# w_down's block sums by accumulating transfers from GpSimd, and another order of the seven products

## The chip, the cores and the metric

The kernel runs on one core of one Trainium2 chip. The metric is the device time of one execution in microseconds; the time before is the median of three runs. A core has five engines that run side by side and wait for each other by semaphores: PE (TensorE, matrix products into PSUM banks), DVE (VectorE), ACT (ScalarE), POOL (GpSimd) and SP (SyncE, which here issues nearly all transfers). PEld is the loading of the stationary operand for PE.

## The reference, cut to what matters

Two layers of a hybrid decoder on a sequence of 512 rows, width 1024, all in float32. Each layer has three parallel branches (a state-space scan, latent attention, a gated delta rule), a gated merge, and then the feed forward, which is what the change touches:

```python
D_MODEL = 1024; SEQ = 512; DEPTH = 2; D_FF = 4 * D_MODEL

    h = x + mixed @ w_out
    f = jnp.square(jax.nn.relu(rmsnorm(h, norm2_g) @ w_up)) @ w_down
    return h + f
```

`w_up` is 1024 x 4096 and `w_down` 4096 x 1024 in each layer.

## The kernel before

Every float32 operand of a product is split into a high part and a rest (`split_half`, lines 170 and 171: ACT casts `whi`, DVE subtracts to get `wlo`), and each product of two blocks is three matmuls (`mm3`, lines 200, 203, 204). The buffers of `whi` and `wlo` are four each, so ACT and DVE run up to four splits ahead of PE, and the cast of a split waits until PE has done with the split four places before it.

The feed forward runs in four quarters of the hidden width, `qd` = 0 to 3, per layer. A quarter is `up(qd)`, four chunks of w_up, and then `seven(...)`: the 512 x 1024 activations times a 1024 x 1024 part of w_down, done with seven products of 512 x 512 blocks instead of eight, with sums of blocks on either side. In w_down's part, the blocks (i, j) are held in tiles `wr00` (called b11), `wr01`, `wr10` (b21), `wr11` (b22), each 128 x 4 x 512, 1 MB. The sums on this side are

- p1 = (0,0) + (0,1), in tile `wp1`, made by DVE in `after(2)` of `seven_weights` (line 1200)
- p3 = (0,1) + (1,1), in place in `wr01`, made by DVE in `after(3)` (line 1200)
- p2 = p1 + (1,1), in two tiles `f` (`halves`, line 1262)
- p4 = p2 + (1,0), written back into `wp1` (`plus4`, line 1275)

Each is two DVE operations of 128 x 1024. `after(c)` is called behind each of up's four chunks and also issues the load of a block on SP (line 1208).

The products are named by their activation operand. Before, their order was a11, a12, s2, s1, s3, s4, a22, and in quarter 3 (`early`) a11, a12, s1, s2, s4, s3, a22. Two pairs of PSUM banks take them: a11, s2, s3 and a22 accumulate in the pair `x`, s1 and s4 in the pair `z`, and a12 has a pair of small banks of its own. After each product DVE adds both of its banks to h or subtracts them (line 1244). A product that goes on in the same pair may start on a bank only when that operation has read it. Within a product the first bank's matmuls and the second's take turns, three each, over four blocks k; so a product is 24 matmuls.

w_out's product of each layer uses `seven` in the same way (with `mid`), and keeps its form.

The program's order on each engine is set by a scheduler that goes by priorities; tiles with one buffer (`wp1`, `wr..`) are given to the next quarter when the last reader is done.

Of the kernel before, what the change touches and what calls it, by code (L numbers as in the profile page):

```python
# [10 lines left out]
F32 = mybir.dt.float32  # L11
# [4 lines left out]
ALU = mybir.AluOpType  # L16
# [4 lines left out]
P = 128  # L21
S = 512
T = S // P
D = 1024
# [31 lines left out]
def hybrid_kernel(ctx, tc, a, out, depth=2, taps=None):  # L56
    nc = tc.nc
    pe, act, dve, pool, sync = nc.tensor, nc.scalar, nc.vector, nc.gpsimd, nc.sync
    uid = itertools.count()

    def mk(pl, shape, dt, tag, bufs=None):
        return pl.tile(shape, dt, tag=tag, name=f"{tag}_{next(uid)}", bufs=bufs)
# [24 lines left out]
    def acc_bank():  # L87
        return mk(ps_acc, [P, 512], F32, "acc")
# [4 lines left out]
    def sm_bank():  # L93
        return mk(ps_sm, [P, 512], F32, "sm")
# [55 lines left out]
    def after_product(i, o):  # L150
        tc.add_manual_dep(i, o.name, order_only, reason="behind a product")

    def behind(key, ins):

        if key in seen_at:
            after_product(ins.ins, seen_at[key])
        else:
            awaiting.setdefault(key, []).append(ins.ins)

    def place(key, ins):  # L160
        seen_at[key] = ins.ins
        for i in awaiting.pop(key, ()):
            after_product(i, ins.ins)

    def split_half(raw, hold=None, first=True, at=None):

        n = raw.shape[1]
        hi, lo = hold or (mk(wp, [P, n], F32R, "whi"), mk(wp, [P, n], F32R, "wlo"))
        with tc.high_priority() if first else nullcontext():
            act.copy(hi, raw)  # L170
            x = dve.tensor_tensor(lo, raw, f32(hi), ALU.subtract)  # L171
            if at:
                behind(at, x)
        return hi, lo
# [116 lines left out]
    def square(o, x, pl, tag, bufs=2, scale=1.0):  # L291
        jk = mk(pl, [P, 512], F32, tag, bufs)[:, : x.shape[-1]]
        act.activation(jk, x, AF.Square, scale=scale, accum_out=o)
# [97 lines left out]
    for ly in range(depth):  # L391
# [206 lines left out]
        for hp in range(4):  # L598
# [61 lines left out]
            for k, wh, wl in wkv:  # L660
                for t in range(T):
                    tok = slice(t * P, (t + 1) * P)
                    o = pss[t // 2][:, t % 2 * 256 : t % 2 * 256 + 256]
                    ah, al, bh, bl = ckh[k][:, tok], ckl[k][:, tok], vcols(wh[:, 0, :]), vcols(wl[:, 0, :])
                    more = t % 2 == 1
                    x = pe.matmul(o, ah, bh, start=k == 0 and not more, stop=False, skip_group_check=more)
# [9 lines left out]
            for j in range(2):  # L676
# [3 lines left out]
                for t in range(T):  # L680
                    n = max(256, (t + 1) * P)
                    tok = slice(t * P, (t + 1) * P)
                    ps = sm_bank()
                    o = ps[:, :n]
# [5 lines left out]
                    n = (t + 1) * P  # L690
                    o = ps[:, :n]
# [9 lines left out]
                for kbs in ((0,), (1,), (3, 2)):  # L701
                    ps = sm_bank()
                    n = 0
# [14 lines left out]
                    for kb, c0, c in parts:  # L718
                        v_h, v_l = (x[:, kb % 2, j, :] for x in vs[kb // 2])
                        o = po[:, c0:]  # L720
# [451 lines left out]
        rows = itertools.count()  # L1172
# [18 lines left out]
        hpl = h_pool.enter_context(tc.tile_pool(name="hp", bufs=1, reuse_waits="tile"))  # L1191
        last = ly == depth - 1
        ssq = [mk(sp, [P, 2], F32, "nss", 4) for _ in range(T)]
        def seven_weights(pl, w2d, r0, sums_at=None):

            b = {}

            def plus(o, x, y):
                for q in (slice(0, 1024), slice(1024, 2048)):
                    z = dve.tensor_tensor(o[:, q], x[:, q], y[:, q], ALU.add)  # L1200
                    if sums_at:
                        behind(sums_at, z)

            def after(c):
                i, j = ((0, 0), (0, 1), (1, 1), (1, 0))[c]
                b[i, j] = mk(pl, [P, 4 * 512], F32, f"wr{i}{j}")
                rows, cols = (slice(o + 512 * e, o + 512 * (e + 1)) for o, e in ((r0, i), (0, j)))
                sync.dma_start(b[i, j].rearrange("p (k n) -> p k n", k=4), w2d[rows, cols].rearrange("(k p) n -> p k n", p=P))
                if c == 2:
                    b["p1"] = mk(pl, [P, 4 * 512], F32, "wp1")  # L1210
                    plus(b["p1"], b[0, 0], b[0, 1])
                if c == 3:
                    plus(b[0, 1], b[0, 1], b[1, 1])

            return b, after

        def seven(pl, ops, b, sq=None, before_last=None, fin=None, nf=4, pre=None, mid=None, prep=None, early=False, tag=None, settled=None, rest=None):

            x, z = ([acc_bank() for _ in range(2)] for _ in range(2))

            def product(ps, n, raw, start, i, j, op, done):

                w = []
                if pre:
                    pre(n)
                rowwise = sq and (done == 2 or (rest and n == "s3"))
                for k in range(4):
                    if pre and n == "s2" and k == 2:
                        pre("s4")
                    w.append(split_half(raw(k)))  # L1230
                    if rowwise:
                        continue
                    for t in range(2):
                        mul(ps, n, w, k, t, start)
                for t in range(2):
                    if rowwise:
                        for k in range(4):
                            mul(ps, n, w, k, t, start)
                    r = 2 * i + t
                    if r == 3 and rest and done == 2:  # L1240
                        return rest(ps[t])
                    hs_ = h[:, r, j * 512 : (j + 1) * 512]
                    with tc.high_priority():
                        place((tag, n, t), dve.tensor_tensor(hs_, hs_, ps[t], op))  # L1244
                    if done and sq:
                        square(sq[r][:, j : j + 1], hs_, pl, "fs", 3 if nf == 4 else 2, D ** -0.5 if settled else 1.0)
                        if settled and i == j:
                            settled(r, j)
                        if done == 2 and fin:
                            fin(r)  # L1250

            def mul(ps, n, w, k, t, start):
                ah, al = (o[:, k % 2 * 256 + t * P : k % 2 * 256 + (t + 1) * P] for o in ops[n][k // 2])
                key = (tag, "s4", 3, 1) if tag and early and n == "s3" and k == 0 else None
                place((tag, n, k, t), mm3(ps[t], ah, al, *w[k], start and k == 0, k == 3, not start, key))

            b11, p3, b21, b22, p1 = (b[n] for n in ((0, 0), (0, 1), (1, 0), (1, 1), "p1"))

            halves = [mk(pl, [P, 2 * S], F32, "f", nf) for _ in range(2)]
            for q, o in enumerate(halves):  # L1260
                cs = slice(q * 1024, (q + 1) * 1024)
                dve.tensor_tensor(o, p1[:, cs], b22[:, cs], ALU.add)
            if prep:
                prep()
            p2 = lambda k: halves[k // 2][:, k % 2 * 512 : k % 2 * 512 + 512]
            of = lambda o: lambda k: o[:, k * 512 : (k + 1) * 512]
            product(x, "a11", of(b11), True, 0, 0, ALU.add, 0)
            if mid:
                mid()
            product([sm_bank() for _ in range(2)], "a12", of(b21), True, 0, 0, ALU.add, 1)  # L1270
            p4 = mk(pl, [P, 4 * 512], F32, "wr00") if mid else p1

            def plus4(q):
                cs = slice(q * 1024, (q + 1) * 1024)
                dve.tensor_tensor(p4[:, cs], halves[q], b21[:, cs], ALU.add)

            later = [lambda: plus4(0), lambda: plus4(1)]
            for n in ("s1", "s2", "s4", "s3") if early else ("s2", "s1", "s3", "s4"):
                if n == "s1":
                    product(z, n, of(p1), True, 1, 1, ALU.add, 0)  # L1280
                if n == "s2":
                    product(x, n, p2, False, 0, 1, ALU.subtract, 0)
                if n == "s3":
                    product(x, n, of(p3), False, 1, 1, ALU.subtract, 1)
                if n == "s4":
                    product(z, n, of(b22), False, 0, 1, ALU.add, 1)
                if later and n in ("s2" if early else "s1", "s4" if early else "s3"):
                    later.pop(0)()
            if before_last:
                before_last()  # L1290
            product(x, "a22", of(p4), False, 1, 0, ALU.add, 2)

        with tc.tile_pool(name="wo", bufs=1, reuse_waits="tile") as wo:
# [12 lines left out]
            b, after = seven_weights(wo, a["w_out"][ly], 0)  # L1306
# [135 lines left out]
        with tc.tile_pool(name="ff", bufs=1, reuse_waits="tile") as fp:  # L1442
# [50 lines left out]

            def down_weights(qd):

                return seven_weights(fp, a["w_down"][ly], qd * D, None if qd else ((ly, "u", 1), 1, 0))

            def ends(qd):

# [21 lines left out]
            for qd in range(4):  # L1521
                b, after = down_weights(qd)
                ops = up(qd, after)
                if qd == 3 and not last:
                    nx = hilo_tags(lp, "x")
                seven(fp, ops, b, **ends(qd))
# [42 lines left out]
```

## Time and profile before

| | |
|---|---|
| median of three runs | 2251.79 us (2250.84 to 2251.88) |
| profiled execution | 2251.54 us, span 2249.7 us |
| granted TensorE clock | 0.999 |
| PE busy | 2240.4 us, 11758 matmuls |
| DVE busy | 1638.8 us |
| ACT busy | 1162.5 us |
| POOL busy | 66.9 us in 84 instructions |
| transfers | 246.95 MB, nearly all by SP's queue q1, 35.9% of the DMA engines' time |
| w_down's blocks (line 1208) | 32 loads of 1024 KB, 5.2 us from issue to landing |
| w_up's blocks (line 179) | 64 loads of 512 KB, 3.6 us |

A row of a group gives line, engine, operation, out<-in, the shape, and the count; behind it the busy time and the mean time of one in ns, or the least, median and longest of one. A row of a time line gives the start, the length (for "x2" from the first start to the last end), and in brackets the idle time before it and what ended it. In the table by stage, each engine's busy time stands with its count, then the clock, the share of the DMA engines and GB/s. The starts of PE's matmuls are exact; their ends are modelled, and they overlap.

### The profile page before, as it was taken

To read this page: it belongs to the slowest core of one execution; us is meant where nothing else is said; L and a number is where in the kernel's file an instruction comes from. 1 tells how busy PE (TensorE), PEld (TensorE's weight loads), DVE (VectorE), ACT (ScalarE), POOL (GpSimd) and SP (SyncE) were. 2 spreads that over 40 slices of the span, in tenths; PEclk is the share of its full clock that TensorE was granted. 3 is DMA by queue.
4 is the path that set the end of the run, shared out by engine and by line. 5 is a ranking of instruction groups with operands and counts; after the bars stand their busy time and mean duration, and the time that the engine had idled before them with its cause. 6 is when DMAs were issued, how large, how long until landed. Compare 5 with 4: busy or idle time off the path is not lost.

```text
span 2249.7 us, 32006 instructions
## 1 busy us (share of the span) xinstructions
PE 2240.4 (100%) x11758; PEld 1866.7 (83%) x11758; DVE 1638.8 (73%) x3259; ACT 1162.5 (52%) x2375; POOL 66.9 (3%) x84
## 2 busy tenths in 40 slices
PE   9999999999999999999999999999999999999998
PEld 8888888888888888888888888888888888888887
DVE  8786567776766777767878775678658668778668
ACT  6555744333543565554656567443345445545546
POOL 1000000000000000000010000000001000000000
PEclk9999999999999999999999999999999999999999
DMA  4333634542325143333133346335422251433231
GB/s 147 96 94 105 196 104 121 142 131 75 85 66 178 57 150 113 96 110 103 45 116 91 90 122 196 103 109 145 123 85 75 66 187 38 169 112 103 85 113 47
DMA packets 221790, 246.95 MB, mean 110 GB/s; under 512 B 34609, under 2 KB 172737, under 8 KB 221633
## 3 DMA queue, kind: packets, MB, share of 16 engines
q1 hardware_dynamic: 221488, 244.65, 35.9%
q8 instruction: 92, 1.51, 0.3%
q14 instruction: 66, 0.53, 0.1%
q10 hardware_dynamic: 144, 0.26, 0.0%
HBM read 225.53 MB, written 11.74 MB: 105 GB/s over the span
## 4 chain that ended last, share of the span: by engine, by line
PE 97%; DVE 2%; POOL 0%; issue 0%; ACT 0%; DMA 0%; SPq 0%; POOLq 0%; ACTq 0%; DVEq 0%
PE acc L200 25%; PE acc L204 24%; PE acc L203 24%; PE sm L204 3%; PE sm L203 3%; PE sm L200 3%; PE sm L706 1%; PE sm L811 1%; PE sm L1093 1%; PE sm L822 1%; PE sm L1119 1%; PE yt L204 1%; PE yt L203 1%; PE yt L200 1%; DVE ckl L748 1%; DVE wlo L171 1%
## 5 line engine op out<-in xcount | busy, mean ns | idle before, releaser
L171 DVE TENSOR_TENSOR wlo<-wraw,whi 128x512 fp32r<-128x512 f32 (+1 forms) x536 | 365.4, 686 | 325.8 <-ACT whi L170 320.4
L170 ACT CAST whi<-wraw 128x512 fp32r<-128x512 f32 (+1 forms) x536 | 329.9, 618 | 517.8 <-PE acc L203 340.7
L200 PE MATMUL acc<-xh,whi 128*128 128x512 f32 (+1 forms) x1344 | 525.4, 391 | 0.0
L204 PE MATMUL acc<-xh,wlo 128*128 128x512 f32 (+1 forms) x1344 | 520.1, 387 | 0.1
L203 PE MATMUL acc<-xl,whi 128*128 128x512 f32 (+1 forms) x1344 | 518.9, 386 | 0.0
L204 PEld LDWEIGHTS acc<-xh,wlo 128*128 128x128 f32 x1344 | 252.7, 188 | 49.6 <-DVE wlo L171 0.5
L200 PEld LDWEIGHTS acc<-xh,whi 128*128 128x128 f32 x1344 | 252.8, 188 | 48.4 <-ACT xh L276 0.5
L203 PEld LDWEIGHTS acc<-xl,whi 128*128 128x128 f32 x1344 | 252.9, 188 | 47.7
L170 ACT CAST whi<-wr 128x512 fp32r<-128x512 f32 x168 | 104.4, 621 | 110.2 <-PE acc L203 47.2
L200 PE MATMUL acc<-yh,whi 128*128 128x512 f32 x384 | 152.7, 401 | 0.0
L203 PE MATMUL acc<-yl,whi 128*128 128x512 f32 x384 | 150.6, 392 | 0.0
L204 PE MATMUL acc<-yh,wlo 128*128 128x512 f32 x384 | 150.1, 391 | 0.0
L171 DVE TENSOR_TENSOR wlo<-wr,whi 128x512 fp32r<-128x512 f32 x168 | 113.1, 686 | 35.9 <-ACT whi L170 34.9
L748 DVE SCALAR_TENSOR_TENSOR ckl<-acc,pc,ckl 128x511 f32<-128x511 f32 (+2 forms) x168 | 120.9, 743 | 18.3 <-ACT ckl L744 10.3
L200 PEld LDWEIGHTS acc<-yh,whi 128*128 128x128 f32 x384 | 71.5, 188 | 16.2 <-ACT yh L276 2.3
L204 PEld LDWEIGHTS acc<-yh,wlo 128*128 128x128 f32 x384 | 72.1, 188 | 14.8
L203 PEld LDWEIGHTS acc<-yl,whi 128*128 128x128 f32 x384 | 72.2, 188 | 13.8
L200 PE MATMUL acc<-whi,xh 128*128 128x512 f32 (+1 forms) x208 | 79.8, 384 | 0.4 <-DVE ckl L748 0.4
L203 PE MATMUL acc<-wlo,xh 128*128 128x512 f32 (+1 forms) x208 | 79.4, 382 | 0.0
L204 PE MATMUL acc<-whi,xl 128*128 128x512 f32 (+1 forms) x208 | 79.2, 381 | 0.0
L1244 DVE TENSOR_TENSOR h<-h,acc 128x512 f32<-128x512 f32 x119 | 76.4, 680 | 0.3 <-PE acc L204 0.3
L495 ACT ACTIVATE eE<-eE,cum 128x128 f32<-128x128 f32 x192 | 63.2, 390 | 24.3 <-DMA eE<-d_c 21.6
(494 smaller groups left out, 4465.0 us busy)
## 6 DMA issues: line engine op xcount, KB each, us to landing
wraw<-in_w_in_dram SPq DMA_DIRECT2D x144, 512.0 KB, 3.7
wraw<-in_w_up_dram SPq DMA_DIRECT2D x64, 512.0 KB, 3.6
wr<-in_w_down_dram SPq DMA_DIRECT2D x32, 1024.0 KB, 5.2
eE<-d_c SPq DMA_DIRECT2D x48, 256.0 KB, 4.5
wraw<-in_w_mla_out_dram SPq DMA_DIRECT2D x16, 512.0 KB, 3.4
eE<-d_e SPq DMA_DIRECT2D x32, 256.0 KB, 3.3
wraw<-in_w_ssd_out_dram SPq DMA_DIRECT2D x16, 512.0 KB, 3.5
wraw<-in_w_gdn_out_dram SPq DMA_DIRECT2D x16, 512.0 KB, 3.6
```

Source lines behind the costliest of these rows:

```text
L170: act.copy(hi, raw)
L171: x = dve.tensor_tensor(lo, raw, f32(hi), ALU.subtract)
L200: x = pe.matmul(o, ah, bh, start=start, stop=False, skip_group_check=more)
L203: pe.matmul(o, ah, bl, start=False, stop=False, skip_group_check=more)
L204: return pe.matmul(o, al, bh, start=False, stop=stop, skip_group_check=more)
L495: act.activation(o[:, i], o[:, i], AF.Relu, scale=-1.0, bias=cum[:, t, h0 + i : h0 + i + 1])
L706: pe.transpose(ps[:, n : n + P], pn[t][:, kb * P : (kb + 1) * P], ident)
L748: dve.scalar_tensor_tensor(acc[:, d:], ps[:, : S - d], taps_[3 - d], acc[:, d:], ALU.mult, ALU.add)
L811: x = pe.matmul(py[64 * i : 64 * i + 64, c * P : (c + 1) * P], xd[:, t, h * 64 : (h + 1) * 64], e2[h // 4][:, h % 4, :], start=True, stop= ...
L822: pe.matmul(po[:, c * P : (c + 1) * P], st[:, c * P : (c + 1) * P], ctl[:, tok], start=True, stop=True)
L1093: x = pe.matmul(pw[:, h * P : (h + 1) * P], Y[:, h, :], r[:, h * P : (h + 1) * P], start=True, stop=True)
L1244: place((tag, n, t), dve.tensor_tensor(hs_, hs_, ps[t], op))
```

## The change

For w_down alone, `chain_weights` takes the place of `seven_weights`, and no sum is made by DVE. `wp1` is loaded from memory with block (0,0) a second time, by SP. GpSimd then issues accumulating transfers, which add a block of w_down from memory onto a tile: (0,1) onto `wp1`, which makes p1; (1,1) onto `wr01`, which makes p3. Inside `seven`, when s1 has been split, (1,1) is added onto `wp1` block by block (four transfers of 128 x 512), which makes p2; when s2 has been split, (1,0) is added in the same way, which makes p4. So p1, p2 and p4 are the same tile at different times, and each addition waits until ACT and DVE have read the block, and the next split waits for the addition.

The order of the products becomes a11, s1, a12, s2, s3, s4, a22, and in quarter 3 a11, s1, a12, s2, s4, s3, a22.

```diff
+        def chain_weights(pl, w2d, r0):
+            b = {"add": lambda k, i, j: pool.dma_start(quarter(b["p1"], k), block(w2d, r0, i, j, k, 1), accum_op=ALU.add)}
+            def after(c):
+                i, j = ((0, 0), (0, 1), (1, 1), (1, 0))[c]
+                b[i, j] = mk(pl, [P, 4 * 512], F32, f"wr{i}{j}")
+                sync.dma_start(quarter(b[i, j], 0, 4), block(w2d, r0, i, j))
+                if c == 0:
+                    b["p1"] = mk(pl, [P, 4 * 512], F32, "wp1")
+                    sync.dma_start(quarter(b["p1"], 0, 4), block(w2d, r0, 0, 0))
+                if c == 1:
+                    pool.dma_start(quarter(b["p1"], 0, 4), block(w2d, r0, 0, 1), accum_op=ALU.add)
+                if c == 2:
+                    pool.dma_start(quarter(b[0, 1], 0, 4), block(w2d, r0, 1, 1), accum_op=ALU.add)
+            return b, after
...
+            if "add" in b:
+                if prep:
+                    prep()
+                product(x, "a11", of(b11), True, 0, 0, ALU.add, 0)
+                product(z, "s1", of(p1), True, 1, 1, ALU.add, 0)
+                for k in range(4):
+                    b["add"](k, 1, 1)
+                product([sm_bank() for _ in range(2)], "a12", of(b21), True, 0, 0, ALU.add, 1)
+                product(x, "s2", of(p1), False, 0, 1, ALU.subtract, 0)
+                for k in range(4):
+                    b["add"](k, 1, 0)
+                for n in ("s4", "s3") if early else ("s3", "s4"):
+                    if n == "s3":
+                        product(x, n, of(p3), False, 1, 1, ALU.subtract, 1)
+                    else:
+                        product(z, n, of(b22), False, 0, 1, ALU.add, 1)
+                if before_last:
+                    before_last()
+                product(x, "a22", of(p1), False, 1, 0, ALU.add, 2)
+                return
...
-                return seven_weights(fp, a["w_down"][ly], qd * D, None if qd else ((ly, "u", 1), 1, 0))
+                return chain_weights(fp, a["w_down"][ly], qd * D)
```

On PE, in quarter 1 of layer 0, at the end of product s2 (operand `mix`): acc_9214 and acc_9215 are the pair `x`, acc_9216 and acc_9217 the pair `z`. Before:

```order
L204 MATMUL acc_9214<-whi_9338,mix_8852 128x512
L200 MATMUL acc_9215<-whi_9338,mix_8851 128x512
L203 MATMUL acc_9215<-wlo_9339,mix_8851 128x512
L204 MATMUL acc_9215<-whi_9338,mix_8852 128x512
L200 MATMUL acc_9216<-whi_9350,yh_1920_8839 128x512
L203 MATMUL acc_9216<-wlo_9351,yh_1920_8839 128x512
```

and now:

```order
L204 MATMUL acc_9214<-whi_9380,mix_8853 128x512
L200 MATMUL acc_9215<-whi_9380,mix_8852 128x512
L203 MATMUL acc_9215<-wlo_9381,mix_8852 128x512
L204 MATMUL acc_9215<-whi_9380,mix_8853 128x512
L200 MATMUL acc_9214<-whi_9396,mix_8854 128x512
L203 MATMUL acc_9214<-wlo_9397,mix_8854 128x512
```

s2 was followed by s1 in the other pair; now s3 follows it in the same pair.

On DVE at the same place, the additions to h and the splits around them (`wr_1971_9023` and `wr_1970_9026` are `wr01`, s3's raw blocks; `wp` is `wp1`). Before:

```order
L171 TENSOR_TENSOR wlo_9361<-wp_1989_9117,whi_9360 128x512
L1275 TENSOR_TENSOR wp_1989_9117<-f_9218,wr_2006_9210 128x1024
L1244 TENSOR_TENSOR h_7368<-h_7368,acc_9214 128x512
L1244 TENSOR_TENSOR h_7368<-h_7368,acc_9215 128x512
L171 TENSOR_TENSOR wlo_9371<-wp_1989_9117,whi_9370 128x512
```

and now:

```order
L171 TENSOR_TENSOR wlo_9407<-wr_1970_9026,whi_9406 128x512
L171 TENSOR_TENSOR wlo_9417<-wr_1970_9026,whi_9416 128x512
L1267 TENSOR_TENSOR h_7368<-h_7368,acc_9214 128x512
L1267 TENSOR_TENSOR h_7368<-h_7368,acc_9215 128x512
L171 TENSOR_TENSOR wlo_9427<-wr_1970_9026,whi_9426 128x512
```

The sum of line 1275 is gone, and ahead of the two additions to h stands the subtraction of the next product's third block.

On SP, the loads for quarter 1 of layer 0, issued while quarter 0's products run. Before:

```order
L1208 DMA wr_1956_8941<-in_w_down_dram 128x4x512
L1208 DMA wr_2006_9210<-in_w_down_dram 128x4x512
L1208 DMA wr_1971_9023<-in_w_down_dram 128x4x512
L1208 DMA wr_1988_9115<-in_w_down_dram 128x4x512
L179 DMA wraw_8946<-in_w_up_dram 128x4x256
```

and now:

```order
L1208 DMA wr_1954_8942<-in_w_down_dram 128x4x512
L1208 DMA wr_2004_9212<-in_w_down_dram 128x4x512
L1208 DMA wr_1970_9026<-in_w_down_dram 128x4x512
L1208 DMA wr_1987_9119<-in_w_down_dram 128x4x512
L1211 DMA wp_1955_8944<-in_w_down_dram 128x4x512
L179 DMA wraw_8949<-in_w_up_dram 128x4x256
```

One load more stands between the blocks of w_down and the next of w_up. GpSimd, which had no instruction here, now has the quarter's ten transfers, 80 in the kernel.

More of the change, by code (lines that the diff above doesn't have):

```diff
@@ L1193, in hybrid_kernel, with quarter, block, seven_weights @@
         ssq = [mk(sp, [P, 2], F32, "nss", 4) for _ in range(T)]
-        def seven_weights(pl, w2d, r0, sums_at=None):
+        def quarter(o, k, n=1):
+            return o[:, k * 512 : (k + n) * 512].rearrange("p (k n) -> p k n", n=512)
+        def block(w2d, r0, i, j, k=0, n=4):
+            rows = slice(r0 + 512 * i + k * P, r0 + 512 * i + (k + n) * P)
+            return w2d[rows, j * 512 : (j + 1) * 512].rearrange("(k p) n -> p k n", p=P)
+        def chain_weights(pl, w2d, r0):
[12 more added lines that the diff above has]
+            return b, after
+        def seven_weights(pl, w2d, r0):
             b = {}
@@ L1199, in plus @@
                 for q in (slice(0, 1024), slice(1024, 2048)):
-                    z = dve.tensor_tensor(o[:, q], x[:, q], y[:, q], ALU.add)
-                    if sums_at:
-                        behind(sums_at, z)
+                    dve.tensor_tensor(o[:, q], x[:, q], y[:, q], ALU.add)
             def after(c):
@@ L1257, in seven @@
             b11, p3, b21, b22, p1 = (b[n] for n in ((0, 0), (0, 1), (1, 0), (1, 1), "p1"))
+            of = lambda o: lambda k: o[:, k * 512 : (k + 1) * 512]
+            if "add" in b:
[18 more added lines that the diff above has]
+                return
             halves = [mk(pl, [P, 2 * S], F32, "f", nf) for _ in range(2)]
@@ L1265, in seven @@
             p2 = lambda k: halves[k // 2][:, k % 2 * 512 : k % 2 * 512 + 512]
-            of = lambda o: lambda k: o[:, k * 512 : (k + 1) * 512]
             product(x, "a11", of(b11), True, 0, 0, ALU.add, 0)
```

## The prediction

> **What bounds the kernel now.** I read the page's busy table first, then the chain of work that ended last, then a table by stage over the stretches that the diff touches.
>
> ```profile
> span 2249.7 us, 32006 instructions
> PE 2240.4 (100%) x11758; PEld 1866.7 (83%) x11758; DVE 1638.8 (73%) x3259; ACT 1162.5 (52%) x2375; POOL 66.9 (3%) x84
> ...
> PE 97%; DVE 2%; POOL 0%; issue 0%; ACT 0%; DMA 0%; SPq 0%; POOLq 0%; ACTq 0%; DVEq 0%
> ```
>
> TensorE is busy all the time and carries 97% of the chain. A busy PE may still hide short waits, so the second table takes the seven products alone: the first and last of the six stretches of quarters 1, 2 and 3 (both layers), and the sum of the six.
>
> ```profile
> 842.90:881.05 38.15, 38.15 (x169) 31.41 (x169) 34.40 (x52) 21.31 (x35) 0.00 (x0) 1.00 0.32 110
> ...
> 2122.30:2160.40 38.10, 38.10 (x169) 31.39 (x168) 34.34 (x52) 21.29 (x35) 0.00 (x0) 1.00 0.32 111
> sum 229.05, PE 229.05 PEld 188.59 DVE 206.45 ACT 127.84 POOL 0.00; mean PE 38.17 PEld 31.43 DVE 34.41 ACT 21.31 POOL 0.00
> ```
>
> PE is busy for 229.05 of 229.05 us at clock 1.00; VectorE is at 90%, ScalarE at 56%, GpSimd idle, the DMA engines at a third. One product is 24 matmuls, a seventh of 38.15 us: 5.45 us. That the matmuls run without gaps shows in their starts, at the place where the products s3 and s4 meet in quarter 1 of layer 0 (first PE, then ACT, then DVE):
>
> ```profile
> 868.68 0.39 PE L204 MATMUL acc<-whi,mix 128*128 128x512 f32 x1
> ...
> 869.36 0.39 PE L204 MATMUL acc<-whi,mix 128*128 128x512 f32 x1
> ...
> 870.04 0.39 PE L204 MATMUL acc<-whi,mix 128*128 128x512 f32 x1
> 870.27 0.39 PE L200 MATMUL acc<-whi,fx 128*128 128x512 f32 x1
> 869.11 0.62 ACT L170 CAST whi<-wr 128x512 fp32r<-128x512 f32 x1 [0.74 <-DVE wlo L171]
> 869.77 0.69 DVE L171 TENSOR_TENSOR wlo<-wr,whi 128x512 fp32r<-128x512 f32 x1 [0.67 <-ACT whi L170]
> 870.38 1.28 DVE L1244 TENSOR_TENSOR h<-h,acc 128x512 f32<-128x512 f32 x2
> L1244 DVE TENSOR_TENSOR h<-h,acc x119: 675/680/686, 740.3 to 2240.6; 128x512 f32<-128x512 f32 x119
> ```
>
> Seven starts from 868.68 to 870.27 are 0.227 us apart. So work taken off VectorE buys nothing unless PE waited for it, and a new wait of PE is paid in full.
>
> **The sums on VectorE that go.** In layer and quarter each, VectorE made p1, p3, p2 and p4 in two halves: 8 operations, 64 over the kernel.
>
> ```profile
> L1200 DVE TENSOR_TENSOR wp<-wr,wr x20: 1217/1218/1226, 715.0 to 2159.4; 128x1024 f32<-128x1024 f32 x20
> L1200 DVE TENSOR_TENSOR wr<-wr,wr x20: 1216/1218/1227, 718.5 to 2164.7; 128x1024 f32<-128x1024 f32 x20
> L1262 DVE TENSOR_TENSOR f<-wp,wr x20: 1215/1218/1222, 721.4 to 2203.7; 128x1024 f32<-128x1024 f32 x20
> L1275 DVE TENSOR_TENSOR wp<-f,wr x16: 1217/1219/1227, 858.6 to 2228.7; 128x1024 f32<-128x1024 f32 x16
> ```
>
> Of these 16 of each fall away (the rest is w_out's): 64 x 1.218 = 78 us of VectorE, worth nothing directly, since it lay beside PE. One place where PE did wait for a crowded VectorE is visible, in s2, at the low part of its second operand pair:
>
> ```profile
> 856.72 0.69 DVE L273 TENSOR_TENSOR mix<-fs,mix 128x512 fp32r<-128x512 f32 x1
> 857.24 0.39 PE L203 MATMUL acc<-wlo,mix 128*128 128x512 f32 x1
> 857.46 0.73 PE L204 MATMUL acc<-whi,mix 128*128 128x512 f32 x2
> ```
>
> VectorE ends at 857.41 and PE goes on at 857.46, so the hand-over of a semaphore takes 0.05 us. The two matmuls last 0.73 instead of 0.39 + 0.227 = 0.62: when a weight load had to wait, the next start is 0.11 us late. With s1 moved ahead, s2 comes one product later and this operand is in time: -0.11 us, in six quarters (I take the other five like this one) -0.6 us.
>
> **The new order of products.** a11, s1, a12, s2, s3, s4, a22 in quarters 0 to 2. s2 and s3 both accumulate in the same two banks, acc_9214 and acc_9215, and now follow each other. VectorE must have added s2's bank to h before s3's first matmul may write it. (In quarter 3 the order is s2, s4, s3, a22, as before from s2 on, and no new neighbours share a bank.) The order has `wlo` of s3's third block ahead of that addition, so the price can be read where the same pattern stands now, in the rows of s3 and s4 above: PE is done with s3's third block (868.68 + 0.39 = 869.07), ACT casts into the freed buffer (869.11 to 869.73), VectorE subtracts (from 869.77), and only then, at 870.38, adds bank 0 to h, until 871.06. The next product's first matmul started at 870.27, in another bank. In the same bank it starts at 871.06 + 0.05 = 871.11: 0.84 us late, and 0.11 for the weight load, 0.95 us. The second bank is added by 871.66, while PE does the three matmuls of the first one (871.11 + 0.11 + 3 x 0.227 = 871.90), so it costs nothing. Six hand-overs: 6 x 0.95 = +5.7 us. Lower end: VectorE is free when bank 0 is complete. Its last matmul is the one at 869.36, which ends at 869.75; the addition would run from 869.79 to 870.47, PE would go on at 870.52, and the wait is 0.25 + 0.11 = 0.36, +2.2 us in all. Upper end: one more VectorE operation of 0.61 us pitch ahead of it: 1.55 each, +9.3 us. I take 0.95, since the order of instructions is the one whose rows these are.
>
> s1 in second place needs its operands where a12 needed its own until now; both are made from the same tile of up, one after the other, and the old order had a12's ready without a wait of PE. I put nothing on it.
>
> **The accumulating transfers.** No row shows one. p1 is summed in place: after s1's split has read block k, GpSimd adds block (1,1) onto it, and s2's split reads it. What counts is the time from that read to the next one. The old rows at these four slots (second product's splits, then the fourth's, then PE's start of the fourth):
>
> ```profile
> 845.78 0.69 DVE L171 TENSOR_TENSOR wlo<-wr,whi 128x512 fp32r<-128x512 f32 x1
> 849.39 1.28 DVE L171 TENSOR_TENSOR wlo<-wr,whi 128x512 fp32r<-128x512 f32 x2
> 855.45 0.62 ACT L170 CAST whi<-wp 128x512 fp32r<-128x512 f32 x1 [0.56 <-PE acc L204]
> 858.23 0.62 ACT L170 CAST whi<-wp 128x512 fp32r<-128x512 f32 x1 [0.79 <-PE acc L204]
> 859.39 0.39 PE L200 MATMUL acc<-whi,yh 128*128 128x512 f32 x1
> ```
>
> Block 0 is read until 845.78 + 0.69 = 846.47 and again from 855.45: 9.0 us. Block 2 is read until 849.39 + 0.68 = 850.07 and again from 858.23: 8.2 us, with nothing moved. PE needs block 0 at 859.3, a split takes 0.62 + 0.69 + 0.1 = 1.4, so the cast may start 2.4 us later before PE waits: 10.6 us in all. For a22, s2's split and the next read are three products apart instead of two: 5.4 us more. The sums made once a quarter during up, (0,1) onto p1 and (1,1) onto p3, have most of up, over 30 us, before a product reads them; they stand on GpSimd's queue behind a22's additions, which are issued as soon as s2 is split. Bounds from rows:
>
> ```profile
> wraw<-in_w_up_dram SPq DMA_DIRECT2D x64, 512.0 KB, 3.6
> wr<-in_w_down_dram SPq DMA_DIRECT2D x32, 1024.0 KB, 5.2
> eE<-d_c SPq DMA_DIRECT2D x48, 256.0 KB, 4.5
> d_e<-eE SPq DMA_DIRECT2D x16, 256.0 KB, 5.2
> DMA to landing us min/median/max: 4.9/5.1/12.6
> L1208 SPq DMA_DIRECT2D wr<-in_w_down_dram x32: 367/368/2376, 797.6 to 2151.6; - x32
> ```
>
> 256 KB loads land after 4.5 us. An addition also writes back, so a load and a store of that size, 4.5 + 5.2 = 9.7 us, is my upper estimate; the longest landing of a w_down block, 12.6, is the far end. An issue took 0.37 us on SP, 2.4 at worst; four of 2.4 in a row reach the fourth block 7 us late at most. I take 4.5 to 9.7, inside 10.6: no cost, with little cover left at the upper end. The Trainium skill, "DMA: Bandwidth & Descriptors", section "Anatomy of one DMA", gives a GpSimd transfer 2.0 us + bytes / 436 GB/s; by it 256 KB would be 2.6 us (an estimate from that page, for a plain copy; no run here shows one), and the sum would be the same.
>
> **SP's queue and the traffic.** SP gets one more 1 MB load (wp) per quarter, behind the four of the next quarter's blocks and ahead of up's loads. It waits for the last read of wp in a22 (first row), then up's load is issued (second), used by a cast at 883.91 when PE frees a buffer, and needed by PE's 892.03:
>
> ```profile
> 877.01 0.69 DVE L171 TENSOR_TENSOR wlo<-wp,whi 128x512 fp32r<-128x512 f32 x1
> 880.19 8.12 SPq L179 DMA_DIRECT2D wraw<-in_w_up_dram  x3
> 883.91 0.62 ACT L170 CAST whi<-wraw 128x512 fp32r<-128x512 f32 x1 [1.94 <-PE yt L203]
> 892.03 0.39 PE L200 MATMUL sm<-xh,whi 128*128 128x512 f32 x1
> ```
>
> wp is issued at 877.7, ahead of 880.19, and lands by 882.9; up's block then at worst 3.6 later, 886.5, against 892.03 - 1.4 = 890.6. No cost, 4 us of cover. In quarter 0 the wp load stands ahead of a block of up's second chunk, which has the same kind of cover. A quarter's bytes rise from 8 to 13 MB: the share 0.32 becomes 0.52, or 0.68 if additions count twice. GpSimd's other work behind the additions, the norms' powers, comes after s3 of quarter 3, two products later: nothing.
>
> **The sum.** +5.7 - 0.6 = +5.1 us on the profiled execution's 2251.54, that is 2256.6; the median of the runs is 0.25 higher, so 2251.8 + 5.1 = 2256.9.
>
> **Rivals.** (1) The hand-over is cheap: VectorE, rid of its sums, adds bank 0 as soon as it is complete. 6 x 0.36 - 0.6 = +1.5, 2253.3 us, no change. For it: VectorE is 10% less loaded. Against: the addition stands behind a subtraction that waits for ACT and PE, not for the sums. It decides below (4.5 + 0.6) / 6 = 0.85 us each, near my 0.95, so no change is not far off.
>
> (2) The additions come late for s2: at 12.6 us, 2.0 over the cover, in 8 quarters 16 us on top, 2273 us. For it: unseen operation, four issues in a row on one queue. Against: 3.3 us would have to be added to the 256 KB load's 4.5 and more. It decides at 10.6 us.
>
> (3) GpSimd cannot issue while VectorE works, which is 90% of these stretches: four issues of 0.37 / 0.1 = 3.7 us; the fourth is out at 846.5 + 14.8 = 861.3 and lands 4.5 later at 865.8, 3.8 us after its last moment (859.3 + 3 x 1.36 - 1.4 = 862.0): 8 x 3.8 = 30, 2287 us. The Trainium skill, "SBUF — State Buffer", section "Who interferes with whom", speaks for this: descriptor writing by GpSimd is held up while VectorE is in a two-port mode. By its own list tensor_tensor has no such mode, and the row agrees: 1.218 us for 1024 columns above, against tensor_scalar's 0.753:
>
> ```profile
> L312 DVE TENSOR_SCALAR f<-h,nrs x10: 745/753/756, 786.6 to 1916.4; 128x1024 f32<-128x1024 f32 x10
> ```
>
> This form stands at the norms alone, not among the products; so I give it little.
>
> **Chances.** Forecast, +4.4 to +5.8: 0.60. Rival 1: 0.17; rival 2: 0.16; rival 3: 0.04; a gain: 0.02; something else slower: 0.01. 0.2%, 4.5 us, is about what a measurement of this kernel can tell from no change; I put a seventh of the forecast's own case below it, since 0.11 us less per hand-over suffices. Slower 0.51 + 0.16 + 0.04 + 0.01 = 0.72, same 0.26, faster 0.02. Range 2253 to 2268: it leaves out some of rival 1 and a gain below, half of rival 2 and rival 3 above; the forecast's own is 2256.2 to 2257.6.
>
> **What would show it.** Right: in quarters 0 to 2 PE idles about 0.85 us at s3's first matmul, released by VectorE's h, six times; s2's 0.11 is gone; quarter 3 has no new wait; whi<-wp of s2 waits for PE, not for a transfer; VectorE's busy time is 78 us less. Wrong: waits of ACT for wp named DMA, PE waiting at s2 in all eight quarters; additions landing later than 10 us; POOL busy for microseconds per issue; up's loads landing after 6 us.

## The result and the profile after

The changed kernel takes 2264.8 us (median of four runs, 2263.66 to 2267.6), the kernel before 2251.84 beside it: ratio 1.006, 95% interval 1.0043 to 1.0078, so 13 us slower. The forecast was 2256.9 in a range of 2253 to 2268: the sign and the range hold, but the loss is two and a half times the 5.1 us that the sum gave.

The page after, busy table, the GpSimd queue and the chain by engine:

```profile
span 2261.9 us, 32211 instructions
PE 2243.4 (99%) x11758; PEld 1866.3 (83%) x11758; DVE 1571.1 (69%) x3195; ACT 1160.7 (51%) x2375; POOL 143.7 (6%) x164
...
q0 software_dynamic: 17664, 33.56, 8.8%
...
PE 94%; DVE 2%; DMA 1%; ACT 1%; issue 0%; POOL 0%; SPq 0%; POOLq 0%; ACTq 0%; DVEq 0%
```

The profiled execution took 2263.66 us, 12.1 more than the one before. VectorE has 67.7 us less to do, GpSimd 76.8 more, and DMA, at 0% of the chain before, now has 1% of it. The view of waits says what PE waited for (total us, times, longest); before the change no such row stood among PE's waits:

```profile
PE acc L200 <- ACT whi L170: 8.6, 8, 2.6
```

Eight waits: six are the hand-overs from s2 to s3, two lie elsewhere. The table by stage of the six sevens with a hand-over, first, last and sum, has PE idle 0.77 us in each, and the DMA engines at 0.77 instead of 0.32 (a word on counting: where the prediction's first tables and their rows say quarters 1, 2 and 3, they count from one; these are qd = 0, 1 and 2, and here quarters are counted from 0):

```profile
846.27:885.22 38.95, 38.18 (x169) 31.31 (x169) 29.90 (x48) 21.30 (x35) 8.18 (x9) 1.00 0.77 181
...
2133.39:2172.34 38.95, 38.18 (x169) 31.30 (x169) 29.89 (x48) 21.30 (x35) 8.24 (x9) 1.00 0.79 180
sum 233.70, PE 229.08 PEld 187.79 DVE 179.35 ACT 127.81 POOL 49.38; mean PE 38.18 PEld 31.30 DVE 29.89 ACT 21.30 POOL 8.23
```

One of the six, in the time line of layer 0, qd = 0:

```profile
867.59 0.69 DVE L171 TENSOR_TENSOR wlo<-wr,whi 128x512 fp32r<-128x512 f32 x1 [0.67 <-ACT whi L170]
867.86 0.39 PE L204 MATMUL acc<-whi,mix 128*128 128x512 f32 x1
868.20 1.28 DVE L1267 TENSOR_TENSOR h<-h,acc 128x512 f32<-128x512 f32 x2
868.29 0.62 ACT L170 CAST whi<-wr 128x512 fp32r<-128x512 f32 x1 [0.74 <-DVE wlo L171]
869.02 0.47 PE L200 MATMUL acc<-whi,mix 128*128 128x512 f32 x1 [0.77 <-ACT whi L170]
```

PE's starts stand 1.16 us apart instead of 0.227, so each hand-over costs 0.93, six of them 5.6 us. The start behind it is late as well, 0.31 us on instead of 0.227. VectorE does what was forecast: it first subtracts for s3's third block (867.59), then adds bank 0 (868.20 to 868.88), and PE goes on. The name in the bracket, ACT's cast, ends at 868.91, 0.03 later than that addition; a bracket names whatever ended last, and this cast is not for PE's next matmul. The experiments below settle which it was.

The other two waits lie in up, quarter 0 of either layer. Layer 0 in before, ACT and then PE:

```profile
816.81 1.14 ACT L170 CAST whi<-wraw 128x512 fp32r<-128x512 f32 x2 [2.69 <-DMA wraw<-in_w_up_dram]
819.61 0.39 PE L204 MATMUL acc<-xh,wlo 128*128 128x512 f32 x1
819.84 0.39 PE L200 MATMUL acc<-xh,whi 128*128 128x512 f32 x1
```

and the same instructions after:

```profile
819.58 0.39 PE L204 MATMUL acc<-xh,wlo 128*128 128x512 f32 x1
821.88 1.14 ACT L170 CAST whi<-wraw 128x512 fp32r<-128x512 f32 x2 [8.94 <-DMA wraw<-in_w_up_dram]
822.54 0.50 PE L200 MATMUL acc<-xh,whi 128*128 128x512 f32 x1 [2.58 <-ACT whi L170]
822.88 0.40 PE L203 MATMUL acc<-xl,whi 128*128 128x512 f32 x1
823.27 0.63 PE L204 MATMUL acc<-xh,wlo 128*128 128x512 f32 x1
823.70 0.63 PE L200 MATMUL acc<-xh,whi 128*128 128x512 f32 x1
824.12 0.63 PE L203 MATMUL acc<-xl,whi 128*128 128x512 f32 x1
```

Before, too, ACT waited for a load of w_up here. Its cast is 5.07 us later now (821.88 less 816.81), and PE 2.73 later than due (822.54 against 819.81): the cover was 2.34 us, and it is gone. Then the matmuls start 0.43 us apart instead of 0.227 for some microseconds: from 823.5 to 826.9 the granted clock is 0.50. The starts in the trace sum to 2.7 us of wait and 2.0 of slow matmuls in layer 0, and 1.5 and 0.6 in layer 1: 6.8 us. With 5.6 for the hand-overs, 0.5 for the late starts behind them and 0.6 less for s2's old wait, which is gone in all six, that makes 12.3 against the 12.1. The rest is scatter: PE's starts in the two profiled executions also differ by 1.4 us one way (before 400 us) and 1.0 the other (1180 to 1400), in stages that the change does not touch.

What holds the loads up shows in the table by stage (the last three columns are the clock, the DMA engines' share and GB/s) and in the landing of w_up's loads from 785 to 835 us. Before:

```profile
808.00:818.00 10.00, 10.00 (x55) 8.68 (x54) 8.99 (x12) 6.82 (x11) 0.00 (x0) 1.00 0.91 329
818.00:828.00 10.00, 10.00 (x46) 8.26 (x44) 5.80 (x10) 5.69 (x9) 0.00 (x0) 1.00 0.34 105
```

```profile
DMA to landing us min/median/max: 3.5/3.9/6.3
```

After, and last the two queues from 815 to 822 (packets, MB, share of the 16 engines):

```profile
808.00:818.00 10.00, 10.00 (x50) 8.42 (x50) 4.02 (x6) 4.19 (x7) 2.71 (x2) 1.00 1.08 291
818.00:828.00 10.00, 7.42 (x25) 5.37 (x24) 1.29 (x2) 1.64 (x3) 0.00 (x0) 0.83 1.09 264
```

```profile
DMA to landing us min/median/max: 3.5/11.1/16.6
```

```profile
q0 software_dynamic: 539, 1.07, 82.4%
q1 hardware_dynamic: 536, 0.54, 28.2%
```

The engines were already nearly full until 818 (0.91) with w_down's first blocks and w_up's; now they are full until 828 (shares go a little over 1, because the records of packets overlap). GpSimd's q0 and SP's q1 deliver packet for packet, 539 to 536, but a packet of an addition (2 KB) takes 0.824 x 16 x 7 us / 539 = 171 ns and one of w_up (1 KB) 59, so w_up gets 77 KB per us, where SP's queue by itself moved 376 GB/s, that is 376 KB per us, of w_down and w_up (the run without the additions, below). The Trainium skill, "DMA: Bandwidth & Descriptors", section "Queues, rings and completion order", says that each DMA engine takes turns between queues packet by packet; the counts agree with equal turns.

### The profile page after: what moved, and what is told of

The parts are those of the page before. It is cut to its first block, busy times and chain, and to the rows that moved or that the text cites. A ratio compares the mean times of both kernels' runs of the same rounds, so it can differ in the third digit from the quotient of the medians.

```text
span 2261.9 us, 32211 instructions
## 1 busy us (share of the span) xinstructions
PE 2243.4 (99%) x11758; PEld 1866.3 (83%) x11758; DVE 1571.1 (69%) x3195; ACT 1160.7 (51%) x2375; POOL 143.7 (6%) x164
## 4 chain that ended last, share of the span: by engine, by line
PE 94%; DVE 2%; DMA 1%; ACT 1%; issue 0%; POOL 0%; SPq 0%; POOLq 0%; ACTq 0%; DVEq 0%
PE acc L200 24%; PE acc L204 23%; PE acc L203 23%; PE sm L204 3%; PE sm L203 3%; PE sm L200 3%; DVE wlo L171 1%; DMA wraw<-in_w_up_dram 1%; ACT whi L170 1%; PE sm L706 1%; PE sm L811 1%; PE sm L1093 1%; PE sm L822 1%; PE yt L204 1%; PE yt L203 1%; PE yt L200 1%
## 5 line engine op out<-in xcount | busy, mean ns | idle before, releaser
L170 ACT CAST whi<-wp 128x512 fp32r<-128x512 f32 x104 | 64.3, 620 | 44.9 <-DVE wlo L171 19.1
L203 PEld LDWEIGHTS acc<-yl,whi 128*128 128x128 f32 x384 | 72.2, 188 | 13.8
L1203 POOL DMA_DIRECT2D wp<-in_w_down_dram x64 | 55.5, 897 | 382.3 <-DVE wlo L171 380.9
```

What stands on the lines that cost most here:

```text
L203: pe.matmul(o, ah, bl, start=False, stop=False, skip_group_check=more)
L1203: b = {"add": lambda k, i, j: pool.dma_start(quarter(b["p1"], k), block(w2d, r0, i, j, k, 1), accum_op=ALU.add)}
```

## The experiments

Each was timed beside the kernel before on the same chip; its difference is to that.

| | median us | to before | ratio, 95% interval |
|---|---|---|---|
| the change | 2264.8 | +13.0 | 1.0060, 1.0043 to 1.0078 |
| e2_q0_dve | 2256.84 | +5.5 | 1.0025, 1.0015 to 1.0034 |
| e3_q0_no_adds | 2256.79 | +5.4 | 1.0025, 1.0016 to 1.0035 |
| e5_q0_plain | 2262.81 | +11.4 | 1.0050, 1.0038 to 1.0063 |
| e4_rows | 2258.92 | +7.5 | 1.0035, 1.0022 to 1.0049 |
| e6_both | 2250.95 | -0.3 | 1.0001, 0.9992 to 1.0010 |
| e1_order_only | 2254.36 | +3.2 | 1.0015, 1.0006 to 1.0024 |
| e7_s1_s2 | 2275.75 | +24.6 | 1.0112, 1.0096 to 1.0127 |
| e8_small_packets | 2263.57 | +12.5 | 1.0055, 1.0043 to 1.0068 |
| e9_one_add | 2259.28 | +8.2 | 1.0040, 1.0026 to 1.0053 |
| e10_later | 2256.83 | +5.8 | 1.0027, 1.0016 to 1.0037 |

**e2: quarter 0's two sums back to DVE.**

```diff
-                return chain_weights(fp, a["w_down"][ly], qd * D)
+                return chain_weights(fp, a["w_down"][ly], qd * D, qd == 0)
...
+                        if c == 2:
+                            behind(((ly, "u", 1), 1, 0), dve.tensor_tensor(b["p1"][:, q], b[0, 0][:, q], b[0, 1][:, q], ALU.add))
+                        if c == 3:
+                            behind(((ly, "u", 1), 1, 0), dve.tensor_tensor(b[0, 1][:, q], b[0, 1][:, q], b[1, 1][:, q], ALU.add))
```

> Quarter 0 of both layers takes p1 and p3 as DVE sums again; the second load of block (0,0) and the two 1 MB additions of that quarter are gone, all else is as in the changed kernel. Theory A (the 7 us beyond the hand-overs come from the two additions, which run beside w_up's loads in quarter 0): PE's waits and the low clock in quarter 0's up go, 2263.7 - 7 = about 2257, w_up's loads land within 6.5 us there, ACT no longer waits for one. Rival B (they come from additions inside the sevens or from the new order of products): stays at 2263 to 2265.

2256.84, as theory A has it, with two details missed: the loads land within 7.3 us, not 6.5, and ACT still waits for two of them, 3.8 us, which PE does not feel. PE's row of waits keeps the hand-overs alone, 4.6 us in six:

```profile
PE acc L200 <- ACT whi L170: 4.6, 6, 0.8
```

```profile
DMA to landing us min/median/max: 3.5/7.2/7.3
```

So 7.5 of the 13.0 us belong to what GpSimd and SP do for p1 and p3 in quarter 0, out of four quarters.

**e3: which of the two, SP's extra load or the additions?** The two additions of quarter 0 are left out, the load stays.

```diff
-                if c == 1:
+                if c == 1 and adds:
                     pool.dma_start(quarter(b["p1"], 0, 4), block(w2d, r0, 0, 1), accum_op=ALU.add)
-                if c == 2:
+                if c == 2 and adds:
                     pool.dma_start(quarter(b[0, 1], 0, 4), block(w2d, r0, 1, 1), accum_op=ALU.add)
```

> The changed kernel without the two 1 MB additions of quarter 0 (p1 and p3 lack one block each there); SP's extra load of (0,0) stays. Theory A (the additions' packets take the DMA engines from w_up's loads): 2257, as with both gone. Rival C (SP's extra 1 MB load, standing ahead of w_up's, is what makes them late): stays at about 2264. Half of each would be about 2260.

2256.79, the same as e2: the load costs nothing, the additions everything. The engines are as full as after the change until 818, and then empty out:

```profile
808.00:818.00 10.00, 10.00 (x52) 8.58 (x52) 5.25 (x8) 6.07 (x10) 0.00 (x0) 1.00 1.07 376
818.00:828.00 10.00, 10.00 (x45) 8.28 (x45) 5.39 (x9) 5.69 (x9) 0.00 (x0) 1.00 0.41 138
```

**e5: is it the adding?** GpSimd's two transfers stay, and overwrite.

```diff
-                    pool.dma_start(quarter(b["p1"], 0, 4), block(w2d, r0, 0, 1), accum_op=ALU.add)
+                    pool.dma_start(quarter(b["p1"], 0, 4), block(w2d, r0, 0, 1), accum_op=op)
```

> The two 1 MB transfers of GpSimd in quarter 0 stay, with the same bytes and packets, but overwrite instead of adding (p1 and p3 are single blocks there). Theory A1 (an accumulating packet is dear, 176 ns for 2 KB against some 85 ns of a plain one): w_up's loads land in about 8 us instead of up to 16.6, and most of the 7 us goes, 2257 to 2259. Theory A2 (any second queue that alternates with SP's takes the share, whatever its packets do): stays above 2261.

2262.81: most of the loss stays without any adding, as A2 has it. One thing in the expectation was wrong. The packets are not the same: a plain transfer of GpSimd goes in packets of 4 KB, 544 for the 2.10 MB, and an addition in 2 KB, 1056. From 808 to 838, this run and then the changed kernel:

```profile
q1 hardware_dynamic: 4163, 5.62, 55.0%
q0 software_dynamic: 544, 2.10, 18.6%
```

```profile
q1 hardware_dynamic: 3892, 5.06, 51.0%
q0 software_dynamic: 1056, 2.10, 38.1%
```

A 4 KB plain packet took 0.186 x 16 x 30 / 544 = 164 ns, a 2 KB adding one 173. So adding doubles the engines' time for the same bytes. Halving it again, as here, hardly helps: the first load of w_up that PE waits for landed 13.3 us after its issue, where A1 had 8 and the change took 12.8. That w_up still waits its turn behind packets as long as before would explain it, but is argued here, not shown: the two queues delivered 150 packets each from 818 to 820, but 339 to 505 from 814 to 819, and no run says why.

**e8: shorter turns.** Each addition of quarter 0 in two halves of the columns.

```diff
+                for e in range(parts):
+                    cs = slice(e * 512 // parts, (e + 1) * 512 // parts)
...
+                        pool.dma_start(quarter(b["p1"], 0, 4)[:, :, cs], block(w2d, r0, 0, 1)[:, :, cs], accum_op=ALU.add)
```

> The changed kernel, but in quarter 0 each of the two 1 MB additions goes as two of half the columns, so that its packets are 1 KB instead of 2 KB; same bytes. If GpSimd's queue and SP's take turns packet by packet (as the trace of the changed kernel has it) and a packet's time goes by its bytes, w_up's loads get about 0.4 of the DMA engines instead of 0.28, land after 10 to 12 us instead of 16.6, and most of the waits in quarter 0's up go: 2257.5 to 2260. If an accumulating packet costs its 176 ns whatever its size, or the share goes by bytes: 2263 to 2266.

2263.57: the theory's time is missed. What it says of the turns came true, from 816 to 820:

```profile
q0 software_dynamic: 481, 0.48, 73.7%
q1 hardware_dynamic: 468, 0.48, 43.7%
```

One for one again, 98 ns for a 1 KB addition packet, w_up's share up from 28.2% to 43.7%. But PE's wait only moved by 11.5 us, to the next loads of w_up:

```profile
831.47 0.39 PE L204 MATMUL acc<-xh,wlo 128*128 128x512 f32 x1
834.05 0.50 PE L200 MATMUL acc<-xh,whi 128*128 128x512 f32 x1 [2.19 <-ACT whi L170]
```

SP's queue shows why. It had issued two loads of w_up, 1.05 MB, at 809.0 and 810.8 (0.55 us later in e8). At 77 KB per us these take 13.6 us, at e8's 0.48 MB in 4 us 8.7, alone at 376 GB/s 2.8 (worked out from the rows). In e8 the first of them landed after 10.1 us instead of 12.8, ACT cast it at 819.74, and PE lost 0.5 us there. But the same bytes in 1 KB packets keep the engines longer, 2112 x 98 = 207 us of engine time against 1056 x 173 = 183, until about 831, and w_down's fourth block stood in SP's queue ahead of the next load of w_up (issued at 821.71), which ACT then had to wait for until 833.38. Whether still smaller packets would help was not run.

**e9: half of it.** p1 keeps its addition in quarter 0, p3 is made by DVE.

```diff
+                if p3_dve:
+                    for q in (slice(0, 1024), slice(1024, 2048)):
+                        if c == 3:
+                            behind(((ly, "u", 1), 1, 0), dve.tensor_tensor(b[0, 1][:, q], b[0, 1][:, q], b[1, 1][:, q], ALU.add))
-                if c == 2:
+                elif c == 2:
```

> In quarter 0 p3 alone is made by DVE; p1 keeps its second load and its 1 MB addition. If the loss goes by how long GpSimd's queue competes with w_up's loads, one addition lasts half as long and the loads have little left to wait for: 2257 to 2260. If any addition at this place costs the full price: about 2263.

2259.28, as the first theory has it: +8.2, that is 2.7 over e2's 5.5, where two additions cost 7.5. Layer 0 keeps one wait of 1.4 us, layer 1 none:

```profile
822.20 0.50 PE L200 MATMUL acc<-xh,whi 128*128 128x512 f32 x1 [1.41 <-ACT whi L170]
```

**e10: the same additions 12 us later.** Nothing is left out; DVE's rewriting of one column holds GpSimd back.

```diff
+                if late and c in (1, 2):
+                    t = b["p1"] if c == 1 else b[0, 1]
+                    behind(((ly, "u", 2), 1, 0), dve.tensor_scalar(t[:, 0:1], t[:, 0:1], 1.0, 0.0, ALU.mult, ALU.add))
```

> All of the changed kernel's transfers stay, but the two 1 MB additions of quarter 0 can start only some 12 us later: ahead of each, DVE rewrites one column of the tile (128 x 1, values unchanged) behind its last split of up's second chunk, and GpSimd waits for that. Theory (the additions cost because they run while SP's backlog of 5 MB of w_down and of w_up's loads fills the DMA engines, until about 818): PE no longer waits in quarter 0's up, 2257, as without them. Rival (the additions cost wherever they meet w_up's loads): the wait moves to up's third or fourth chunk, 2261 to 2266. If p1 then comes too late for s1, PE waits there, about 2260.

2256.83, as with no additions at all. GpSimd issues at 823 instead of 808 and 812, the engines are full from 828 to 838, and PE never waits there:

```profile
823.09 1.48 POOL L1216 DMA_DIRECT2D wp<-in_w_down_dram  x1 [22.84 <-DVE wr L1214]
824.05 1.85 POOL L1218 DMA_DIRECT2D wr<-in_w_down_dram  x1
```

```profile
828.00:838.00 10.00, 10.00 (x46) 8.27 (x45) 5.27 (x9) 6.31 (x11) 0.00 (x0) 1.00 1.11 229
```

So the loss of quarter 0 is a matter of the moment: the additions do harm while SP's backlog is still in the engines. The run tests the rival only in part, because GpSimd now issues behind SP's last load of w_up for this quarter (822.3); the next, at 827.8, takes 10.8 us to land, but is for quarter 1 and nobody waits for it. The changed kernel's own quarter 1 does test it. There the addition for p1 (issued at 890.7, when wp's load and the blocks ahead of it have landed) runs beside w_up's loads, which land within 7.0 us instead of 3.8 before; ACT waits 5.5 us for one of them, and PE is busy without a gap.

**e4: s2 bank by bank.**

```diff
-                rowwise = sq and (done == 2 or (rest and n == "s3"))
+                rowwise = (sq and (done == 2 or (rest and n == "s3"))) or (n == "s2" and nf == 4 and not early)
```

> The changed kernel with the matmuls of s2 taken bank by bank in quarters 0 to 2, so that its first bank is complete half a product before the second. Theory (the hand-over in one pair of banks costs 0.93 us six times): these waits go, 2263.7 - 5.6 = about 2258, and the 7 us in quarter 0's up stay. Rival (the wait only moves, to s2's second bank or to the splits, which a bank-by-bank product needs sooner): 2262 to 2265.

2258.92, so 5.5 us less than the change, and the six waits are gone from PE's row; what is left are the two of quarter 0:

```profile
PE acc L200 <- ACT whi L170: 4.4, 2, 3.4
```

**e6: both remedies.** e2's and e4's edits together.

> Quarter 0's p1 and p3 by DVE, and s2 bank by bank in quarters 0 to 2, in one kernel; the other additions stay with GpSimd. If the two causes are all there is, and add up: 2263.7 - 7 - 5.6 = about 2251, as before the change (2250.5 to 2252.5). If a third cost is left, for instance additions inside the sevens that come late: above 2254. If VectorE's relief of some 60 us were worth anything, below 2250.

2250.95, no difference from before (0.9992 to 1.0010). The two causes add up to all of the loss, and GpSimd's other additions cost nothing that shows beside the interval. Nor does VectorE's relief bring anything: it is busy 59 us less than before the change,

```profile
PE 2239.0 (100%) x11758; PEld 1865.3 (83%) x11758; DVE 1579.4 (70%) x3203; ACT 1162.1 (52%) x2375; POOL 138.9 (6%) x160
```

and the time is the same. It is the best of the versions run, and no better than leaving the change out.

**e1: the order alone.** All sums by DVE as before, the products in the new order; DVE's additions to h stand ahead of the split of s3's third block.

```diff
+            if new:
+                product(z, "s1", of(p1), True, 1, 1, ALU.add, 0)
             product([sm_bank() for _ in range(2)], "a12", of(b21), True, 0, 0, ALU.add, 1)
...
```

> The new order of products alone: all sums by DVE as before, no transfer of GpSimd. DVE's order at the hand-over is another here: the additions to h stand ahead of the split of s3's third block. Theory (the hand-over is paid by what stands ahead of the addition on DVE): 0.4 us each instead of 0.93, six times, less 0.6 for s2's old wait, about 2253 to 2254.5. Rival (the same pair costs 0.93 whatever stands there): 2256.8. Rival (the order costs nothing, the transfers make all of the 12 us): 2251.8.

2254.36, +3.2. Without that split ahead of the addition the hand-over is cheaper, and its bracket names VectorE:

```profile
864.35 1.28 DVE L1269 TENSOR_TENSOR h<-h,acc 128x512 f32<-128x512 f32 x2
864.44 0.39 PE L204 MATMUL acc<-whi,mix 128*128 128x512 f32 x1
...
865.17 0.47 PE L200 MATMUL acc<-whi,mix 128*128 128x512 f32 x1 [0.34 <-DVE h L1269]
```

865.17 less 864.44 is 0.73: 0.50 each, 3.0 us for six (the late start behind each, 0.08, and s2's old 0.11, gone here too, nearly cancel). The price of the pair of banks depends on what stands ahead of the addition on VectorE, and the transfers are not needed for it.

**e7: is the cover of the additions in the seven real?** The order a11, s1, s2, a12 leaves them 5.45 us less.

```diff
-                product([sm_bank() for _ in range(2)], "a12", of(b21), True, 0, 0, ALU.add, 1)
                 product(x, "s2", of(p1), False, 0, 1, ALU.subtract, 0)
+                product([sm_bank() for _ in range(2)], "a12", of(b21), True, 0, 0, ALU.add, 1)
```

> Order a11, s1, s2, a12, s3, s4, a22: s2 and s3 no longer follow each other in one pair, so the six hand-overs of 0.93 us go, -5.6 us; but p1's block is read again one product sooner, and the cover of the additions inside the seven falls from 10.6 us until PE waits to 10.6 - 5.45 = 5.2. If an addition takes 6 to 7 us from the last read until the block can be split (256 KB landing in 5.6, and the issue), s2 is 1 to 2 us late in 8 quarters: 2263.7 - 5.6 + 8 to 16 = 2266 to 2274. If it is done in 5.2, 2258.

2275.75, just above the expected span. The additions themselves land as fast, but now ACT waits for them 23 times (view of the line that issues them; in the changed kernel the list of who waited is empty):

```profile
who waited for it (us, times):
  ACT whi L170: 30.3, 23
...
DMA to landing us min/median/max: 4.0/4.8/6.6
```

and PE waits for what is queued on ACT and DVE behind those casts, the split of s2's own operand, in all eight quarters, up to 2.6 us:

```profile
PE acc L204 <- DVE mix L273: 11.7, 8, 2.6
```

At s2 PE's starts are 13.8 us late in sum, the hand-overs' 5.6 are saved, and up loses about 1.5 more than after the change; some 2 us lie in small pitches and are not settled.

## Why the prediction was right, and where it was not

**Right: the seven products.** Of PE's saturation: 59 us off VectorE are worth nothing (e6). Of the hand-over: 0.95 us was forecast from the rows of s3 and s4, 0.93 measured (1.01 with the late start behind it), six times, at the instruction named and by the chain named (subtraction, then addition, then PE). s2's 0.11 is gone. Rival 1 asked for an addition that does not stand behind the subtraction; e1 is that case, 0.50 instead of the 0.36 worked out. The additions in the sevens landed after 4.0 to 6.9 us, 5.6 in the median, which is the estimate of 4.5 to 9.7 but for its lower end, and inside the cover of 10.6; e7 shows that the cover was needed, which is what rival 2 turned on. Rival 3 is out: 128 x 512 issues took 0.86 us on a VectorE 77% busy there, and none was waited for. The 2.6 us for 256 KB that the prediction worked out from the Trainium skill, "DMA: Bandwidth & Descriptors", section "Anatomy of one DMA", is less than the least landing, 4.0; but that is a plain copy's figure, and here an addition was measured.

**Wrong: "In quarter 0 the wp load stands ahead of a block of up's second chunk, which has the same kind of cover."** That sentence carried a row of quarter 1 over to quarter 0, and it asked of the wrong transfer. The load was harmless (e3). GpSimd's sums of 1 MB were costed by when a product reads them, "over 30 us" later, and not by whom they disturb on the way. The cover of w_up's loads in quarter 0 was 2.34 us, and the trace before had it: ACT idle 2.69 us for a load at 816.81, and the DMA engines at 0.91 from 808 to 818. In the later quarters the same sums cost nothing. This step is 6.8 us of the profiled execution's 12.1, and nearly all of the 7.0 by which that passes the forecast of 5.1. The list of wrong signs did name it: loads of up landing after 6 us (one took 6.3 before the change already). That 2264.8 still lies within 2253 to 2268 is luck. The forecast's own cases end at 2257.6, and the room above them was kept for rival 2, additions late for s2, which did not happen.

**Sizes that were off, at no cost.** VectorE's busy time falls by 67.7 instead of 78 us: neighbours on VectorE overlap by 0.08 us at either end (0.69 long, 0.61 apart in the rows), so a sum that falls away saves less than its 1.218. With an overlap at both ends of all 64 it would be 64 x 1.058 = 67.7, an estimate that fits better than it should, since not every sum had a neighbour on both sides. The share of the DMA engines in the seven rose to 0.77, not to 0.68 at most. An addition does take the engines about twice as long for its bytes: in the first seven GpSimd's queue has 43.1% for 2.82 MB, SP's 33.2% for 4.18. But the prediction spread the quarter's additions evenly, and most of their bytes move within the seven. The wp load took 9.5 us to land in the median, not 5.2, and in the later quarters PE waited for none of up's loads behind it.

## What to carry to other kernels

A transfer has two prices: when its own data is needed, and whom it holds up in the DMA engines while it runs. For the second, look at the stage where the engines' share is near 1 already and a cast waits for a load, even if PE does not wait yet; a second queue placed there took half the turns. Before reordering products, see which pair of accumulators the neighbours share, and what stands on VectorE ahead of the operation that frees it.

## What the runs showed of the hardware

An adding packet of 2 KB took 171 to 173 ns of a DMA engine, as long as a plain one of 4 KB from the same queue (164); of 1 KB, 98. The issue of a 128 x 512 addition kept GpSimd 0.86 us, of 1 MB 1.3.

A long wait of PE can cost more than its length. After waits of 2.7, 3.0, 3.2 and 3.5 us in quarter 0 of layer 0 (the change, e7, e5, e4) the matmuls stood 0.43 us apart for 3.6 to 6.4 us, a further 1.8 to 3.0 us each; after waits of 1.2 to 2.4 in up (e8 and e9 among them) the extra was 0.4 to 0.6. Length alone does not decide: one wait of 2.8 us at s2 in e7 had no slow matmuls behind it. The Trainium skill, "TensorE: Matmul & The Clock Gate", section "What's actually happening", has the half clock follow an idle window of about 3.4 us, in windows that run freely; here a wait of 2.7 was enough once and one of 2.8 was not. The granted clock in the traces was 0.50 for 3.41 us after each of the first kind (6.83 in e7), and in all four runs from the same moment, 819.20 us after it first became 1.00, which is 240 times 3.413. Counted in stretches of such a grid, the wait of 2.8 fell into two, at most 1.5 us of idling in either; the one of 2.7 lay almost whole in one, 2.5 us of 3.41. No clean threshold comes out: in e5 the stretch ahead of the slow one had 1.6 us of idling, and one with 1.7 in layer 1 of e7 had no slow one behind it.
